# A gated-linear-attention and dilated-window decoder trunk: the elementwise work of the seven-product pairs on VectorE alone

## The chip, the cores and the metric

The kernel runs on one core of one Trainium2 chip. The metric is the device time of one execution in microseconds (us), as the median of several runs. Profiles are of one execution, taken by the hardware profiler. The engines are called PE (TensorE, the matrix engine; PEld is its loading of weights), DVE (VectorE), ACT (ScalarE), POOL (GpSimd) and SP (SyncE, which here only issues DMAs).

## The reference

The program is a decoder trunk of two layers for one sequence of 1024 tokens with 1024 features, in float32. The first layer is gated linear attention with four heads, the second is dilated sliding-window attention with eight query heads in three groups of window and dilation over one shared K and V. Cut to what matters here:

```
proj = x @ w_in                        # layer 1: q, k, v, g and the gates' low rank part
o = gla_chunked(q, k, v, log_a)
x = layer_norm(ALPHA * x + (rms(o) * norm_g * silu(g)) @ w_out)
k, v = split(x @ w_kv); k = rope(k)    # shared by all of layer 2
q, g = split(x @ w_in2); q = rope(q)   # three groups x eight heads of 128
o = softmax-weighted sum over the groups of dilated_window_attention(q, k, v)
x = layer_norm(ALPHA * x + (o * silu(g)) @ w_out2)
```

The matrix products that the change concerns are some of the projections `x @ w`: q and k of all heads of layer 1, and in layer 2 the shared K and most of the q.

## The kernel before

**Precision.** TensorE takes float32 operands in a rounded form (fp32r) at a higher pace than whole float32. A projection is therefore done with split operands: every operand x is stored as a rounded high part and a low part x - high, and a product is three matmuls: high x high, high x low and low x high. ScalarE makes the high part (`split_hi`), and a subtraction makes the low part (`split_lo`, which may go to VectorE or GpSimd). For some weights the low part is made otherwise: ScalarE writes the negative high part, and a DMA issued by GpSimd adds the weight to it in memory (`accum_op`).

**Seven products for a pair.** Two projections of the same input that belong together (q and k of a head, or two K or q heads) are one pair. Such a pair is a 2 x 2 block product: two output blocks of features by two halves of the sequence, over two halves of the input features. It is computed with seven block products in place of eight (P1 to P7), at the price of sums of weight blocks before, and additions of results after. The sums of the input blocks (T1 to T4) are made once per layer. For each pair, `load_pair` (from line 783) loads the two weights (tiles `wf`), forms four sums of weight blocks (tiles `sum`: t1 to t4, by `total`), and splits them with `put` into high parts (`wh`) and low parts (`wl`; the last pair of tiles is called `s`). `seven` (from line 831) issues the 84 matmuls of 128x512 into four PSUM tiles (all called `sev` in the profile), copies P1 and P7 out with ScalarE (u1 and u2, in the profile `u<-sev`), because P2 and P4 are added onto the same banks afterwards, and forms the results: with VectorE `f += P5`, `u += P6`, `c21 = u + (P7 + P4)` and `u += P3`, and last `f = u + f` (`u<-u,u`), on whichever of VectorE and GpSimd the planner picks. There are four pairs in layer 1 and fourteen in layer 2 (three for K, eleven for q; list `EARLY`). In layer 2 each result is turned by `rope` (tiles `t` and `pair`), in layer 1 it is stored to DRAM (`c`, `u`).

**What sets the order.** The program is written as a list of operations, and a planner (class `Sched`, `order`, from line 270) plays them through before anything is issued: it has a price for every operation on every engine, knows which tiles each reads and writes, how many buffers a tile has and a priority, and takes the operation that can start first. `S.vector`, `S.scalar` and so on are one engine; `S.vp` leaves the planner the choice between VectorE and GpSimd, `S.va` between VectorE and ScalarE, `S.vap` among all three. Each engine then runs its own queue in the planned order, and waits at an operation until what it reads is there. An operation that moves to another engine therefore changes the planned times of what follows, and with them the order of the queues and the later choices for other `S.vp` and `S.vap` operations. All instructions have one line in the profile (line 469, where the planner issues them), so they are told apart by their tiles.

**The rest.** After the pairs of layer 2 comes the attention of the eight heads (tiles `P`, `PT`, `lv`, `po`, `nat`, `og`), in which TensorE also does the remaining q projections and the g projections (`acc`), then the output projection with the layer norm.

Of the kernel before, what the change touches and what calls it, by code (L numbers as in the profile page):

```python
# [7 lines left out]
F32 = mybir.dt.float32  # L8
# [116 lines left out]
class Pool:  # L125
# [6 lines left out]
    def tile(self, shape, dtype, name, tag=None, bufs=1):  # L132
        b = Buf(self, shape, dtype, name, tag or name, bufs)
        self.bufs_made.append(b)
        cols = int(_np.prod(shape[1:]))
        if self.space == "DRAM":
            idx = _np.arange(int(_np.prod(shape))).reshape(shape)
        else:

            idx = _np.broadcast_to(_np.arange(cols).reshape((1,) + tuple(shape[1:])), shape)  # L140
        return View(b, idx)
# [484 lines left out]
def trunk(tc, xT, xp, wP, wA, wA12, wAv3, w2, wO, wK, wV0, wV12, wB, wOB, par_d,  # L626
          ident_d, lmask_d, cos_d, sin_d, bmask_d, rmask_d, tri_d, lnr_d, out):
    S = Sched(tc, lat=LAT, pad=PAD)
# [8 lines left out]
    t2 = S.pool("t2", after=(tq,))  # L637
    t0 = S.pool("t0", side="right")
    t1 = S.pool("t1", side="right", after=(t0,))
# [3 lines left out]
    def split_hi(dst, src):  # L643
        S.scalar.activation(dst, src, AF.Copy)

    def split_lo(dst, src, hi):
        S.vp.tensor_sub(dst, src, hi.bitcast(F32))

    def page(pool, dt, name):
        return pool.tile([128, T], dt, name=name, tag="pg", bufs=16)  # L650
# [4 lines left out]
    def hs(half):  # L655
        return slice(half * 512, half * 512 + 512)
# [112 lines left out]
    def og_page(kt, pool):  # L769
        while kt >= len(ogs):  # L770
            n = len(ogs)
            a = page(pool, FR, f"ogh{n}")
            b = page(pool, FR, f"ogl{n}")
            ogs.append((a, b))
        return ogs[kt]

    def pairs(xs, quarter, tile):
        L, R = slice(0, 512), slice(512, 1024)

        def four(x):  # L780
            return x.rearrange("p (k c) -> p k c", k=4)

        def load_pair(src, first=False):
            with S.later(-WEIGHTS):
                a, b = (wts.tile([128, 1024], F32, name="wf", bufs=2) for _ in range(2))
                for x, w in ((a, src[0]), (b, src[1])):
                    S.sync.dma_start(x.rearrange("p (k c) -> p k c", k=NK), w)

                def halves():
                    hi, lo = (wts.tile([128, 1024], FR, name=n, bufs=3) for n in ("wh", "wl"))  # L790
                    return [(hi[:, c], lo[:, c]) for c in (L, R)]

                def put(w, x, more=None):
                    hi, lo = w
                    split_hi(hi, x)
                    if more is None:
                        split_lo(lo, x, hi)
                    else:
                        S.scalar.activation(lo, x, AF.Copy, scale=-1.0)
                        S.gpsimd.dma_start(four(lo), more, accum_op=OP.add)  # L800
                    return four(hi), four(lo)

                def total(op, x, y):
                    t = tile("sum", "a")
                    op(t, x, y)
                    return t

                w0, w1 = halves()
                a11 = put(w0, a[:, L], None if first else src[0][:, 0:4])
                t3 = total(S.vp.tensor_sub, a[:, L], b[:, L])  # L810
                s3 = put(w1, t3)
                w0, w1 = halves()
                a12 = put(w0, a[:, R], None if first else src[0][:, 4:8])
                a22 = put(w1, b[:, R], None if first else src[1][:, 4:8])
                w0, w1 = halves()
                t1 = total(S.vp.tensor_add, b[:, L], b[:, R])
                s1 = put(w0, t1)
                t2 = total(S.vp.tensor_sub, t1, a[:, L])
                s2 = put(w1, t2)
                t4 = total(S.vp.tensor_sub, a[:, R], t2)  # L820
                s4 = put([tile("s4", "d", FR) for _ in range(2)], t4)
            return dict(P1=a11, P2=a12, P4=a22, P7=s3, P5=s1, P6=s2, P3=s4)

        def pure(k0, h):
            return [(xs[k0 + k][0][:, hs(h)], xs[k0 + k][1][:, hs(h)]) for k in range(4)]

        MOVING = dict(P1=lambda: pure(0, 0), P2=lambda: pure(4, 0), P3=lambda: pure(4, 1),
                      **{p: lambda n=n: [quarter(n, k) for k in range(4)]
                         for p, n in (("P4", "T4"), ("P5", "T1"), ("P6", "T2"), ("P7", "T3"))})

        def seven(w, evac):
            banks = {}

            def prod(p, bank):
                first = bank not in banks
                if first:
                    tag = {"a": "acc", "b": "lv", "c": "po", "d": "acc"}[bank]
                    banks[bank] = ps.tile([128, 512], F32, name="sev", tag=tag, bufs=2)
                acc = banks[bank]
                hi, lo = w[p]  # L840
                for k, (xh, xl) in enumerate(MOVING[p]()):
                    with S.group():
                        S.tensor.matmul(acc, hi[:, k, :], xh, start=first and k == 0, stop=False, skip_group_check=True)
                        S.tensor.matmul(acc, hi[:, k, :], xl, start=False, stop=False, skip_group_check=True)
                        S.tensor.matmul(acc, lo[:, k, :], xh, start=False, stop=(k == 3), skip_group_check=True)
                return acc

            def late():
                return S.later(-EVAC)

            acc = prod("P1", "a")
            u = tile("u1", "a")
            with S.later(-WEIGHTS - EVAC):
                S.scalar.copy(u, acc)
            acc = prod("P7", "b")
            f = tile("u2", "a")
            with S.later(-WEIGHTS - EVAC):
                S.scalar.copy(f, acc)
            acc = prod("P2", "a")
            with late():  # L860
                evac(0, 0, acc)
            prod("P4", "b")
            acc = prod("P5", "c")
            with late():
                S.vector.tensor_add(f, f, acc)
            acc = prod("P6", "d")
            with late():
                S.vector.tensor_add(u, u, acc)
                c21 = tile("c", "a")
                S.vector.tensor_add(c21, u, banks["b"])  # L870
                evac(1, 0, c21)
                S.vp.tensor_add(f, u, f)
                evac(1, 1, f)
            acc = prod("P3", "c")
            with late():
                S.vector.tensor_add(u, u, acc)
                evac(0, 1, u)

        return load_pair, seven

    def natural(x):
# [981 lines left out]
    def quarter(name, k):  # L1863
        pg = QS.setdefault((name, k), page(p0, FR, f"{name}{k}"))
        return pg[:, 0:512], pg[:, 512:1024]
# [44 lines left out]
    for half in range(2):  # L1910
        for kt in range(4, 6):
            load_og(ogB[kt], kt, p1, lambda: small("ogf", "a", NA), (half,))
        for u in (6, 7):
            hi, lo = og_page(u, p1)
# [8 lines left out]
    for kt in range(NK):  # L1923
        wf = wts.tile([128, 1024], F32, name="wf", bufs=2)
        q = p1 if kt < 4 else p0
        hi, lo = page(q, FR, "woh"), page(q, FR, "wol")
# [116 lines left out]
```

## Time and profile before

| | |
|---|---|
| median of 3 runs | 1106.04 us (1105.65 to 1107.79) |
| the profiled execution | 1106.84 us |
| its span, first to last instruction | 1105.1 us |
| mean granted TensorE clock | 0.999 |
| busy: PE / DVE / ACT / POOL | 1092.1 / 884.8 / 653.4 / 215.5 us |

A line of a group reads: line, engine, operation, out<-in by the program's names (buffer numbers left out), shapes, count | busy time in us, mean ns of one | idle time of the engine just before them, and what ended it. `wl<-sum,wh` is the low part of a sum of weights, `u<-u,u` the last addition. A line of the timeline has the start in us from the span's start, the duration in us, the engine and the operation, and in brackets for how long the engine was idle before it and what it waited for. A line of the waits has the engine and the tile that waited, what it waited for, the total in us, how often, and the longest.

### The profile page before, as it was taken

How to read it: one execution, taken by the hardware profiler on the slowest of the kernel's cores; microseconds unless marked ns; L12 is line 12 of the kernel's file. 1: busy time of each engine (PE TensorE's matmuls, PEld its weight loads, DVE VectorE, ACT ScalarE, POOL GpSimd, SP SyncE). 2: the span in 40 equal slices, each digit the busy share in tenths (PEclk: the TensorE clock that was granted, in tenths of full speed). 3: DMA queues.
4: the chain of work that ended last, by engine and by line, in shares of the span. 5: the costliest groups of instructions: out<-in, count | busy, mean ns of one | idle time of the engine just before them, and what ended most of it. 6: DMA issues, size and time to landing. Idle time of an engine off the chain costs nothing.

```text
span 1105.1 us, 20222 instructions
## 1 busy us (share of the span) xinstructions
PE 1092.1 (99%) x7532; PEld 932.7 (84%) x7532; DVE 884.8 (80%) x1786; ACT 653.4 (59%) x1330; POOL 215.5 (19%) x247
## 2 busy tenths in 40 slices
PE   9999999999999999999999999999999999999997
PEld 9978888888888888888887888888888898888886
DVE  5886879999567589888888989885588878786578
ACT  5565545666455255656666666675677787763252
POOL 0121100000013021012223322111133553340010
PEclk9999999999999999999999999999999999999999
DMA  8467783134362455767756776678533553241644
GB/s 301 140 211 201 242 290 124 65 134 165 107 202 90 148 166 196 228 175 159 183 151 178 184 203 169 186 189 273 167 97 124 194 160 103 99 152 64 188 136 176
DMA packets 92626, 185.70 MB, mean 168 GB/s; under 512 B 16912, under 2 KB 38032, under 8 KB 92528
## 3 DMA queue, kind: packets, MB, share of 16 engines
q1 hardware_dynamic: 84320, 167.11, 46.1%
q0 software_dynamic: 8208, 17.31, 9.2%
q8 instruction: 59, 0.97, 0.4%
q14 instruction: 39, 0.32, 0.1%
HBM read 134.57 MB, written 47.71 MB: 165 GB/s over the span
## 4 chain that ended last, share of the span: by engine, by line
PE 89%; DVE 5%; DMA 3%; issue 1%; ACT 1%; POOL 0%; DVEq 0%; POOLq 0%; ACTq 0%; SPq 0%
PE acc L469 28%; PE sev L469 26%; PE po L469 12%; PE lv L469 9%; PE vac L469 8%; PE ms L469 4%; PE pro L469 3%; DMA wf<-in_wB 1%; DMA wf<-in_wOB 1%; DVE pair L469 1%; DMA wf<-in_wA 1%; DVE sum L469 1%; DVE wl L469 1%; DVE P L469 1%; DVE xg L469 1%
## 5 line engine op out<-in xcount | busy, mean ns | idle before, releaser
L469 ACT ACTIVATE wh<-wf 128x1024 fp32r<-128x1024 f32 (+3 forms) x118 | 99.5, 844 | 98.6 <-PE acc L469 37.0
L469 PE MATMUL sev<-T,wh 128*128 128x512 f32 x448 | 137.8, 389 | 0.0
L469 PEld LDWEIGHTS sev<-T,wh 128*128 128x128 f32 x448 | 84.1, 188 | 17.4
L469 PE MATMUL sev<-T,wl 128*128 128x512 f32 x224 | 87.2, 389 | 0.0
L469 PE MATMUL lv<-K,Q 128*64 128x64 f32 (+2 forms) x512 | 72.1, 287 | 0.6 <-DVE nat L469 0.5
L469 PE MATMUL acc<-x1h,wh 128*128 128x512 f32 x160 | 71.2, 445 | 0.0
L469 DVE TENSOR_TENSOR wl<-wf,wh 128x1024 fp32r<-128x1024 f32 (+3 forms) x55 | 62.2, 1135 | 10.9 <-ACT wh L469 10.7
L469 POOL DMA_DIRECT2D wl<-in_wB x42 | 36.9, 882 | 169.4 <-ACT wl L469 152.2
L469 DVE CUSTOM_DVE_ANT_0 P<-lv,bmask 128x256 f32<-128x256 f32 (+1 forms) x128 | 47.6, 379 | 19.4 <-PE lv L469 16.9
L469 PE MATMUL acc<-x1h,wl 128*128 128x512 f32 x160 | 62.8, 392 | 0.0
L469 PE MATMUL acc<-x1l,wh 128*128 128x512 f32 x160 | 62.5, 391 | 0.0
L469 POOL TENSOR_TENSOR wl<-wf,wh 128x1024 fp32r<-128x1024 f32 x7 | 16.7, 2388 | 234.3 <-PE ms L469 195.4
L469 DVE TENSOR_TENSOR pair<-t,t 128x512 f32<-128x512 f32 x56 | 60.3, 1083 | 0.3
L469 PEld LDWEIGHTS lv<-K,Q 128*128 128x128 f32 (+1 forms) x512 | 51.8, 164 | 8.8 <-DVE nat L469 1.0
L469 DVE TENSOR_TENSOR t<-t,sinT 128x512 f32<-128x512 f32 x60 | 43.1, 720 | 15.0 <-ACT t L469 14.8
L469 ACT ACTIVATE P<-P,sts 128x64 f32<-128x64 f32 (+2 forms) x128 | 49.8, 391 | 8.5 <-DVE sts L469 7.3
L469 PE MATMUL acc<-xh,wh 128*128 128x512 f32 x128 | 52.6, 411 | 0.0
L469 DVE TENSOR_TENSOR u<-u,sev 128x512 f32<-128x512 f32 x54 | 36.5, 683 | 17.8 <-PE sev L469 17.5
L469 PE MATMUL acc<-xh,wl 128*128 128x512 f32 x128 | 50.1, 391 | 0.0
L469 PE MATMUL acc<-xl,wh 128*128 128x512 f32 x128 | 49.9, 390 | 0.0
L469 PEld LDWEIGHTS sev<-T,wl 128*128 128x128 f32 x224 | 42.0, 188 | 8.8
L469 ACT ACTIVATE t<-u 64x512 f32<-64x512 f32 x56 | 35.4, 632 | 20.8 <-DVE u L469 17.3
(346 smaller groups left out, 3379.9 us busy)
## 6 DMA issues: line engine op xcount, KB each, us to landing
wf<-in_wB SPq DMA_DIRECT2D x32, 512.0 KB, 6.2
wf<-in_wA SPq DMA_DIRECT2D x24, 512.0 KB, 4.1
qd<-pair SPq DMA_DIRECT2D x22, 512.0 KB, 3.2
Q<-qd SPq DMA_DIRECT2D x22, 512.0 KB, 7.9
wl<-in_wB POOLq DMA_DIRECT2D x33, 256.0 KB, 7.1
wf<-in_wO SPq DMA_DIRECT2D x16, 512.0 KB, 3.3
wf<-in_wOB SPq DMA_DIRECT2D x16, 512.0 KB, 3.7
wf<-in_wV SPq DMA_DIRECT2D x10, 512.0 KB, 4.2
```

The costliest lines, as they stand in the source:

```text
L469: getattr(handle[o.eng], meth)(*[conv(a) for a in args], **{k: conv(v) for k, v in kw.items()})
```

## The change

Six lines in `load_pair` and `seven` name VectorE in place of the choice between VectorE and GpSimd; in a pair they issue nine operations: the four sums of weights, the low parts that are made by a subtraction (the four of the sums; in a layer's first pair three more, of plain weights), and the final addition `f = u + f`. The other uses of `S.vp` and of `split_lo` in the program stay. The planner, its prices and everything else are the same; the planner runs anew on the changed list.

```diff
                     if more is None:
-                        split_lo(lo, x, hi)
+                        S.vector.tensor_sub(lo, x, hi.bitcast(F32))
...
-                t3 = total(S.vp.tensor_sub, a[:, L], b[:, L])
+                t3 = total(S.vector.tensor_sub, a[:, L], b[:, L])
...
-                t1 = total(S.vp.tensor_add, b[:, L], b[:, R])
+                t1 = total(S.vector.tensor_add, b[:, L], b[:, R])
                 s1 = put(w0, t1)
-                t2 = total(S.vp.tensor_sub, t1, a[:, L])
+                t2 = total(S.vector.tensor_sub, t1, a[:, L])
                 s2 = put(w1, t2)
-                t4 = total(S.vp.tensor_sub, a[:, R], t2)
+                t4 = total(S.vector.tensor_sub, a[:, R], t2)
...
-                S.vp.tensor_add(f, u, f)
+                S.vector.tensor_add(f, u, f)
```

Both programs hold the same operations, the same DMAs and the same 84 matmuls a pair. What moves is the engine of some of them and, through the planner, the order of the queues. First GpSimd's queue in the pairs of the second layer, before; `in_wK` and `in_wB` are the weights of K and of q, the DMAs are those that add onto low parts, and `u`, `wl`, `sum` and `s` are operations that the diff touches:

```order
L469 TENSOR_TENSOR wl<-sum,wh 128x512 x2
L469 TENSOR_TENSOR sum<-wf 128x512
L469 DMA wl<-in_wB 128x512 x3
L469 TENSOR_TENSOR u_6372<-u_6367,u_6372 128x512
L469 DMA wl<-in_wB 128x512 x3
L469 TENSOR_TENSOR s_6625<-sum,s_6607 128x512
```

These six rows are a piece from the fifth to the seventh pair. GpSimd's queue after, over all fourteen pairs and what stands next to them:

```order
L469 TENSOR_TENSOR T_5414<-rt,T_5414 128x512
L469 DMA wl<-in_wK 128x512 x6
L469 DMA wl<-in_wB 128x512 x33
L469 DMA wl<-in_wB 128x1024
L469 MEMSET diag 128x512 x2
L469 DMA wl<-in_wB 128x1024 x2
```

The computation between the DMAs has left the queue. ScalarE's queue in the sixth pair of the second layer, before; `u_6367` and `u_6372` are the copies of P1 and P7, `wh<-sum` is the rounding of a sum of the next pair's weights:

```order
L469 ACTIVATE wh<-wf 128x512
L469 ACTIVATE wl<-wf 128x512
L469 ACTIVATE wh<-sum 128x512
L469 ACTIVATE u_6367<-sev 128x512
L469 ACTIVATE u_6372<-sev 128x512
L469 ACTIVATE s_6385<-sum 128x512
```

The rounding stands ahead of the copies. The same place after, where the copies are `u_6363` and `u_6371`:

```order
L469 ACTIVATE wh<-wf 128x512
L469 ACTIVATE wl<-wf 128x512
L469 ACTIVATE u_6363<-sev 128x512
L469 ACTIVATE u_6371<-sev 128x512
L469 ACTIVATE wh<-sum 128x512
L469 ACTIVATE s_6377<-sum 128x512
```

The copies have moved ahead of the rounding. In the fourth pair of the second layer it went the other way; ScalarE's queue there before, with the copies `u_6010` and `u_6016`:

```order
L469 ACTIVATE wh<-wf 128x512
L469 ACTIVATE wl<-wf 128x512
L469 ACTIVATE u_6010<-sev 128x512
L469 ACTIVATE u_6016<-sev 128x512
L469 ACTIVATE wh<-sum 128x512
L469 ACTIVATE s_6023<-sum 128x512
```

The copies stand first. The same place after, where the copies are `u_6023` and `u_6027` and `t_5991` belongs to the rope of the pair before:

```order
L469 ACTIVATE wh<-wf 128x512
L469 ACTIVATE wl<-wf 128x512
L469 ACTIVATE wh<-sum 128x512
L469 ACTIVATE t_5991<-u_5834 64x512
L469 ACTIVATE u_6023<-sev 128x512
L469 ACTIVATE u_6027<-sev 128x512
L469 ACTIVATE s_6034<-sum 128x512
```

The rounding, and a piece of the rope, have moved ahead of the copies.

## The prediction, made before the changed kernel ran

> **What bounds the kernel now.** I read the page's first part, then TensorE's waits, then busy time by stretches, then the groups of GpSimd and VectorE, and last the timeline around the one wait of TensorE that the change can touch. The page:
>
> ```profile
> span 1105.1 us, 20222 instructions
> PE 1092.1 (99%) x7532; PEld 932.7 (84%) x7532; DVE 884.8 (80%) x1786; ACT 653.4 (59%) x1330; POOL 215.5 (19%) x247
> ```
>
> TensorE is busy for 1092.1 of 1105.1 us. Moving elementwise work among the other engines can therefore win at most the 13.0 us in which TensorE is not busy. All its waits, from the table of waits:
>
> ```profile
> PE lv L469 <- issue: 1.4, 2, 1.1
> PE pro L469 <- DVE zero L469: 1.3, 1, 1.3
> PE sev L469 <- ACT u L469: 1.2, 1, 1.2
> PE vac L469 <- issue: 0.7, 1, 0.7
> PE lv L469 <- DVE nat L469: 0.5, 1, 0.5
> PE sev L469 <- DVE tT L469: 0.5, 1, 0.5
> ```
>
> They sum to 5.6 us, and the stretches place most of the rest:
>
> ```profile
> 490.00:760.00 270.00, 268.77 (x1188) 221.87 (x1187) 233.24 (x325) 171.30 (x292) 64.81 (x63) 1.00 0.71 185
> 800.00:1000.00 200.00, 199.38 (x1439) 178.62 (x1436) 162.89 (x659) 148.48 (x507) 84.41 (x132) 1.00 0.41 129
> 1000.00:1105.00 105.00, 97.69 (x460) 81.56 (x459) 73.25 (x110) 37.25 (x54) 5.08 (x3) 0.99 0.45 148
> ```
>
> The columns are length, then busy time and count of PE, PEld, DVE, ACT and POOL, then clock and DMA. The last 105 us hold 7.3 us without TensorE, mostly the final layer norm and store, which run after the last seven-product. From 490 to 760 us, where the fourteen pairs of the second layer run, TensorE is idle for 1.2 us in all. The attention (800 to 1000 us) has 0.6 us.
>
> Matmul busy time could hide slow matmuls, so I also count them, in slices of 20 us:
>
> ```profile
> 560.00:580.00 20.00, 20.00 (x90) 16.57 (x89) 16.00 (x24) 12.87 (x23) 5.13 (x5) 1.00 0.56 146
> 580.00:600.00 20.00, 18.83 (x84) 15.22 (x83) 18.19 (x23) 12.64 (x22) 6.89 (x6) 1.00 0.63 172
> 600.00:620.00 20.00, 20.00 (x90) 16.57 (x89) 17.64 (x26) 13.06 (x23) 4.67 (x5) 1.00 0.77 191
> ```
>
> A full slice issues 90 matmuls, one in 0.222 us. The middle slice issues 84, which makes the loss 6 x 0.222 = 1.33 us, against 1.17 us of missing busy time.
>
> **Where that wait comes from.** The timeline of four engines, each line with its start, its duration and what it waited for:
>
> ```profile
> 584.62 2.89 POOL L469 TENSOR_TENSOR wl<-sum,wh 128x512 fp32r<-128x512 f32 x2
> 584.94 3.55 DVE L469 TENSOR_TENSOR pair<-t,t 128x512 f32<-128x512 f32 x1
> 592.43 0.69 DVE L469 TENSOR_TENSOR sum<-wf 128x512 f32<-128x512 f32 x1 [1.43 <-DMA wf<-in_wB]
> 592.54 1.74 POOL L469 TENSOR_TENSOR sum<-wf 128x512 f32<-128x512 f32 x1 [5.03 <-DMA wf<-in_wB]
> 594.31 0.63 ACT L469 ACTIVATE wh<-sum 128x512 fp32r<-128x512 f32 x1 [1.55 <-POOL sum L469]
> 594.85 1.07 ACT L469 ACTIVATE u<-sev 128x512 f32<-128x512 f32 x2
> 593.92 0.39 PE L469 MATMUL sev<-T,wl 128*128 128x512 f32 x1
> 595.48 0.50 PE L469 MATMUL sev<-x1h,wh 128*128 128x512 f32 x1 [1.17 <-ACT u L469]
> ```
>
> The weights land at about 592.4 us. VectorE forms one sum in 0.69 us and GpSimd the other in 1.74 us. ScalarE stands at the rounding of GpSimd's sum (wh), and behind it in its queue are the two copies (u) that take P1 and P7 out of their banks. P2 adds onto P1's bank, so TensorE waits 1.17 us for the copy. This is the only place in the trace where a GpSimd operation of this code reaches TensorE.
>
> **The change part by part.** First, what leaves GpSimd. These groups of the whole program are the code that the diff touches:
>
> ```profile
> L469 POOL TENSOR_TENSOR u<-u,u 128x512 f32<-128x512 f32 x8 | 12.0, 1506 | 14.7 <-DVE u L469 14.7
> L469 POOL TENSOR_TENSOR wl<-sum,wh 128x512 fp32r<-128x512 f32 x8 | 11.1, 1442 | 4.9 <-ACT wh L469 4.9
> L469 POOL TENSOR_TENSOR sum<-wf 128x512 f32<-128x512 f32 x3 | 4.5, 1511 | 13.0 <-DMA wf<-in_wB 5.0 <-issue 4.4 <-DMA mq<-c 3.5
> L469 POOL TENSOR_TENSOR s<-sum,s 128x512 fp32r<-128x512 f32 x2 | 3.0, 1498 | 2.2 <-ACT s L469 2.2
> L469 POOL TENSOR_TENSOR sum<-wf,sum 128x512 f32<-128x512 f32 x2 | 2.6, 1301 | 13.9 <-DVE sum L469 13.9
> L469 POOL TENSOR_TENSOR sum<-sum,wf 128x512 f32<-128x512 f32 x1 | 1.3, 1292 | 5.4 <-DVE sum L469 5.4
> ```
>
> That is 8 + 8 + 3 + 2 + 2 + 1 = 24 operations and 34.5 us of GpSimd; the planner had given VectorE all others already. What they cost on VectorE, and what VectorE pays for their neighbourhood today:
>
> ```profile
> L469 DVE TENSOR_TENSOR pair<-t,t 128x512 f32<-128x512 f32 x56 | 60.3, 1083 | 0.3
> L469 DVE TENSOR_TENSOR t<-t,sinT 128x512 f32<-128x512 f32 x60 | 43.1, 720 | 15.0 <-ACT t L469 14.8
> L469 DVE TENSOR_TENSOR wl<-sum,wh 128x512 fp32r<-128x512 f32 x46 | 37.1, 825 | 1.2 <-ACT wh L469 1.2
> L469 DVE TENSOR_TENSOR sum<-wf 128x512 f32<-128x512 f32 x33 | 23.6, 755 | 9.2 <-DMA wf<-in_wB 7.1 <-DMA wf<-in_wK 1.4 <-DMA wf<-in_wA 0.7
> L469 DVE TENSOR_TENSOR t<-u,cosT 128x512 f32<-128x512 f32 x28 | 20.4, 728 | 0.0
> L469 DVE TENSOR_TENSOR t<-c,cosT 128x512 f32<-128x512 f32 x14 | 11.5, 822 | 0.2
> L469 DVE TENSOR_TENSOR c<-u,sev 128x512 f32<-128x512 f32 x18 | 12.3, 683 | 2.6 <-PE sev L469 2.2
> ```
>
> The last group reads PSUM and takes 683 ns; that is the undisturbed price, so the additions cost 24 x 0.683 = 16.4 us. The groups with both inputs in SBUF have higher means. The pair<-t,t of the timeline shows why: it began during GpSimd's wl operations (584.62 to 587.51 us), ended about 1.0 us after them, and took 3.55 us instead of 1.08 us. The excess over 683 ns is 46 x 0.142 = 6.5 (wl), 33 x 0.072 = 2.4 (sum), 14 x 0.139 = 1.9, 60 x 0.037 = 2.2 and 28 x 0.045 = 1.3 us, and 2.5 us for that one pair: 16.8 us. If all of it goes, VectorE's load changes by 16.4 - 16.8 = -0.4 us; if none goes, by +16.4 us. I take -0.4, since the pair's row shows the cause directly. Even +16.4 us would fit: from 490 to 760 us, where most of it falls, VectorE is idle for 36.8 us. So VectorE does not become the bound. The Trainium skill's "Perfetto Trace Analysis" (Optimizing Scalar/DVE Operations) speaks against the change as far as VectorE is saturated: then giving work to GpSimd may make sense. The trace has VectorE at 233.24 of 270 us there, which is not saturated; if it were, the 16.4 us would come on top of the time. The Trainium skill's "SBUF — State Buffer" (SBUF: two separate sides) says that a VectorE operation with two SBUF inputs and a reading GpSimd operation exclude each other for a whole instruction; the pair's row agrees. By that rule VectorE could get back as much as the 34.5 us that GpSimd held, and would end 18 us lighter; as VectorE is not the bound, the time would be the same.
>
> GpSimd's issues of the accumulating DMAs (wl<-in_w...), which bring the other low parts, now wait behind no computation: in the rows of its queue shown with the change, everything between the DMAs is gone. I cost this at nothing: TensorE never waits for such a DMA in its table, and an earlier issue only lengthens the cover.
>
> Second, the planner moves ScalarE's queue. In the sixth pair of the second layer, the place of the 1.17 us wait, the rows with the change show the copies (u_6367 before, u_6363 after) behind the rounding before, and ahead of it after. So this wait goes whole: -1.2 us (between -1.33 by the count and 0 if something else is late there). But over the fourteen pairs the rounding stands ahead of the copies 9 times before and 10 times after: the fourth, eighth and tenth pair lose the good order that the third and sixth gain. What the rounding waits for there is a landing:
>
> ```profile
> DVE sum L469 <- DMA wf<-in_wB: 7.1, 5, 1.7
> ```
>
> VectorE waited five times for late weights, and one of the five reached TensorE, with GpSimd's slow sum on top. Each of the ten places can thus cost between 0 and 1.2 us. I take a third of one such wait, +0.4 us: the sum itself is now 0.69 instead of 1.74 us, so the landing that cost 1.2 us before would cost 1.2 - 1.0 = 0.2 us at such a place now.
>
> Third, the attention. The shifted start makes the planner deal again there: GpSimd has 107 instead of 91 of the scalings and maskings of P (P and PT below), 8 instead of 12 of og<-og,sg and 5 instead of 7 full-width wl, and VectorE and ScalarE what is left.
>
> ```profile
> L469 POOL TENSOR_SCALAR P<-P,ew 128x256 f32<-128x256 f32 x27 | 14.1, 551 | 4.0 <-DVE ew L469 4.0
> L469 POOL TENSOR_SCALAR P<-P,cw 128x256 f32<-128x256 f32 x9 | 5.7, 637 | 0.0
> L469 POOL TENSOR_TENSOR PT<-P,ident 128x256 f32<-128x256 f32 x9 | 7.5, 843 | 2.8 <-PE po L469 2.6
> ```
>
> Sixteen more at 0.55 to 0.84 us are 9 to 13 us, on an engine that is idle for 115 of these 200 us. TensorE's idle time there was 0.6 us, so little can be won; 1.5 us either way is my estimate from the six waits above, whose size is 0.5 to 1.4 us. I take 0.
>
> Sum: -1.2 + 0.4 + 0 = -0.8 us. The profiled execution took 1106.84 us, 1.74 us above its span and 0.8 us above the median of 1106.04 us; it becomes 1106.0 us, and the median 1105.2 us. The runs before spread over 2.1 us, so about 0.2% (2.2 us) is what can be told from no change, and the forecast is: no change.
>
> **The rivals.** *Slower: late weights meet the new queues.* If three of the ten places where a rounding stands ahead of the copies get a wait of 1.2 us, and the old one goes, that is -1.2 + 3.6 = +2.4 us: 1108.4 us. It decides from the third such wait on. For it: five late landings in this trace, and three pairs that changed to the bad order. Against it: four of the five cost nothing, and every sum now takes 0.69 us. A new wait for P in several of the eight attention rounds would act on top.
>
> *Faster: hidden stalls go too.* If besides the 1.2 us the waits for nat and tT (0.5 us each) go, that is 2.2 us, and any relief in the attention takes it beyond: 1103.6 us. For it: VectorE loses operations of up to 3.55 us that made its queue late. Against it: TensorE's count is full in the slices beside the wait.
>
> *The change does nothing.* The old wait could stay with another cause: 1106.0 us, within the forecast's band.
>
> **How the numbers follow.** No change within 0.2%: 0.70, of which the forecast's own mechanism has 0.55 and "does nothing" 0.15. Faster: 0.15, since nearly every recoverable wait must go. Slower: 0.15, since three new waits are needed, and the queues of the pairs and of the attention have both moved. The range runs from 1103.3 us (faster rival with 0.3 us more) to 1107.8 us (two new waits of 1.2 us, 1107.2, and 0.6 us of the attention's doubt); it leaves out about 1 in 10 at each end.
>
> **What would show it.** Right: POOL has none of the six groups; wl<-sum and sum<-wf on VectorE have means near 685 ns; VectorE's total stays within some 5 us of 884.8 us, while GpSimd's falls by about 30 us; TensorE shows no wait for u near 594 us and its busy total stays within 2 us of 1092.1 us. Wrong: waits "PE sev <- ACT u" at three or more places, a slice of the pairs with under 88 matmuls, or waits of lv or po for POOL in the attention.

## The result and the profile after

The kernel after takes 1113.38 us (median of 5 runs, 1111.4 to 1113.84), the kernel before 1106.06 us in the same series. The ratio is 1.0064, with a 95% interval of 1.0052 to 1.0075: slower, where no change was forecast. The same code measured again later (e11 below) gave 1111.08 us and 1.0051 (1.0036 to 1.0067). So the change costs 5 to 7 us.

The page of the profiled execution, which took 1113.31 us:

```profile
span 1111.5 us, 20202 instructions
PE 1092.7 (98%) x7532; PEld 932.0 (84%) x7532; DVE 878.4 (79%) x1795; ACT 653.9 (59%) x1334; POOL 182.6 (16%) x234
```

The work is about what the prediction said: TensorE has the same 1092.7 us (1092.1 before), GpSimd lost 32.9 us, and VectorE, with 24 operations more to do in the pairs, is 6.4 us lighter. What grew is the time in which TensorE is idle, from 13.0 to 18.8 us. Its largest waits now:

```profile
PE sev L469 <- ACT u L469: 3.9, 3, 2.8
PE lv L469 <- issue: 3.3, 3, 1.6
...
PE vac L469 <- issue: 1.0, 1, 1.0
```

The wait for the copies `u` was one of 1.2 us; now there are three, and one is 2.8 us. Busy time by stretches (the columns are those of the prediction's stretches), first two of before that the prediction did not read:

```profile
62.00:135.00 73.00, 72.52 (x319) 59.33 (x317) 57.45 (x86) 43.91 (x72) 15.80 (x16) 1.00 0.72 208
135.00:310.00 175.00, 172.97 (x2561) 146.33 (x2559) 147.34 (x252) 97.34 (x138) 2.37 (x1) 1.00 0.42 149
```

And of after:

```profile
62.00:135.00 73.00, 70.18 (x308) 57.32 (x307) 54.23 (x86) 41.98 (x68) 10.08 (x12) 1.00 0.69 202
135.00:310.00 175.00, 170.74 (x2549) 144.37 (x2548) 146.22 (x249) 95.96 (x134) 2.37 (x1) 1.00 0.42 148
490.00:760.00 270.00, 268.56 (x1201) 221.63 (x1200) 231.17 (x345) 171.78 (x296) 36.70 (x43) 1.00 0.71 183
```

The loss is in layer 1: TensorE has 2.3 us less in the stretch of the four pairs (62 to 135 us) and 2.2 us less in the one behind it. The second figure belongs for the most part to this one execution: in e11, the same code, TensorE has 172.89 us there, 0.1 us less than before. The stretch on which the prediction spent its words, 490 to 760 us, moved by 0.2 us. That the neighbours of GpSimd got shorter shows in VectorE's groups of after:

```profile
L469 DVE TENSOR_TENSOR pair<-t,t 128x512 f32<-128x512 f32 x56 | 56.1, 1003 | 0.5
L469 DVE TENSOR_TENSOR wl<-sum,wh 128x512 fp32r<-128x512 f32 x54 | 36.5, 705 | 3.6 <-ACT wh L469 3.6
L469 DVE TENSOR_TENSOR sum<-wf 128x512 f32<-128x512 f32 x36 | 24.4, 717 | 11.5 <-DMA wf<-in_wB 8.3 <-DMA wf<-in_wK 3.2
```

The means fell from 1083, 825 and 755 ns, and eight low parts more cost 0.6 us less in sum (37.1 to 36.5).

**Where the 2.8 us come from.** The second pair of layer 1, in the timeline of before:

```profile
69.62 0.42 SPq L469 DMA_DIRECT2D mq<-c  x1
...
74.53 0.75 DVE L469 TENSOR_SCALAR mn<-z,par 128x512 f32<-128x512 f32 x1 [0.47 <-ACT sp L469]
75.20 0.68 DVE L469 TENSOR_TENSOR u<-u,sev 128x512 f32<-128x512 f32 x1
...
77.04 1.50 POOL L469 TENSOR_TENSOR sum<-wf 128x512 f32<-128x512 f32 x1 [3.54 <-DMA mq<-c]
78.17 0.60 ACT L469 ACTIVATE u<-sev 128x512 f32<-128x512 f32 x1 [1.49 <-DMA mq<-u]
```

And of after:

```profile
68.53 0.33 SPq L469 DMA_DIRECT2D mq<-c  x1
...
76.66 0.75 DVE L469 TENSOR_SCALAR mn<-z,par 128x512 f32<-128x512 f32 x1 [3.47 <-DMA mq<-c]
77.33 0.68 DVE L469 TENSOR_TENSOR sum<-wf 128x512 f32<-128x512 f32 x1
77.93 0.68 DVE L469 TENSOR_TENSOR u<-u,sev 128x512 f32<-128x512 f32 x1
...
80.91 0.68 DVE L469 TENSOR_TENSOR_SCAN b<-smask,mn 128x256 f32<-128x256 f32 x1
81.69 0.60 ACT L469 ACTIVATE u<-sev 128x512 f32<-128x512 f32 x1 [6.43 <-DVE b L469]
82.34 0.50 PE L469 MATMUL sev<-xh,wh 128*128 128x512 f32 x1 [2.82 <-ACT u L469]
```

The tiles `sum`, `u`, `c`, `sp` and `mn` of layer 1 share nine buffers (kind `a`). One of them is held by `c` until its store `mq<-c` has landed, which by the rows takes 7.4 us from its issue before and 8.1 us after. Before, GpSimd's sum got this buffer, waited 3.54 us for it, and had nothing behind it that anybody missed. After, the same wait (3.47 us) is at the head of VectorE's queue, at `mn`, a step of the gates. Behind it stand the moved sum, the evacuation of P3 (`u<-u,sev`, at 77.93 instead of 75.20 us) and the scans `b`. The copy of the next pair's P1 (`u<-sev` on ScalarE) now gets the buffer of a `mn`, which a scan frees, and starts 3.5 us later than before. TensorE stands still for it.

**The second place.** A burst of small matmuls in the attention of layer 1 (64 rows `lv<-X` in the order, 128 records in the profile), in TensorE's timeline of before:

```profile
182.18 1.41 PE L469 MATMUL lv<-X 128*32 128x32 f32 x128
```

And of after, where the planner has put the burst ahead of two triples of `acc` matmuls that it stood behind:

```profile
183.13 1.20 PE L469 MATMUL lv<-X 128*32 128x32 f32 x108
185.43 0.38 PE L469 MATMUL lv<-X 128*32 128x32 f32 x20 [1.10 <-issue]
```

TensorE stops after 108 of the 128 for 1.10 us and waits for nothing that the profile shows.

**Layer 2.** In the sixth pair the copies stand ahead of the rounding, and the wait near 594 us is gone. In the twelfth the rounding waits for a sum and the copies wait behind it. There ScalarE has the rounding ahead of the copies in both kernels; what differs is VectorE's queue. Before, the sums came ahead of a step of the rope:

```profile
708.17 1.34 DVE L469 TENSOR_TENSOR sum<-wf 128x512 f32<-128x512 f32 x2
709.38 0.74 DVE L469 TENSOR_TENSOR t<-t,sinT 128x512 f32<-128x512 f32 x1
```

After, VectorE works without a break and reaches them only behind that step and a `pair<-t,t`, 1.8 us of work:

```profile
712.75 0.74 DVE L469 TENSOR_TENSOR t<-t,sinT 128x512 f32<-128x512 f32 x1
713.53 1.11 DVE L469 TENSOR_TENSOR pair<-t,t 128x512 f32<-128x512 f32 x1
714.56 1.29 DVE L469 TENSOR_TENSOR sum<-wf 128x512 f32<-128x512 f32 x2
715.28 0.63 ACT L469 ACTIVATE wh<-sum 128x512 fp32r<-128x512 f32 x1 [2.07 <-DVE sum L469]
716.45 1.06 ACT L469 ACTIVATE u<-sev 128x512 f32<-128x512 f32 x2
717.07 0.50 PE L469 MATMUL sev<-x1h,wh 128*128 128x512 f32 x1 [0.61 <-ACT u L469]
```

All this is put together in a table of how far TensorE is behind the kernel before. Both traces hold 7532 matmuls; an entry is the start of the n-th in the trace named, less the start of the n-th in the trace of before, where n is the matmul that starts at the time above the column in before. A jump between two columns is time lost in between; the end is that of the last matmul. A TensorE that is late can find a later wait shorter (e1 between 592 and 607 us), so the jumps of a row do not simply add up.

| us | 73 | 90 | 192 | 497 | 592 | 607 | 757 | 990 | end |
|---|---|---|---|---|---|---|---|---|---|
| after | -1.1 | 2.0 | 3.6 | 4.4 | 5.6 | 4.1 | 5.4 | 6.6 | 6.5 |
| after again (e11) | -1.0 | 2.5 | 2.7 | 2.8 | 2.9 | 1.4 | 2.6 | 3.8 | 3.3 |
| layer 1 only (e1) | -1.2 | 3.9 | 4.8 | 4.5 | 4.6 | 3.5 | 3.4 | 3.4 | 2.9 |
| layer 2 only (e2) | -0.3 | -0.3 | -0.6 | -0.1 | 0.4 | -1.1 | 0.1 | 0.9 | 1.3 |
| order of before (e3) | 0.2 | 3.3 | 3.3 | 3.6 | 3.5 | 2.4 | 2.1 | 2.0 | 2.1 |
| all but one sum (e4) | -1.0 | -0.2 | -0.5 | 2.5 | 2.7 | 1.5 | 1.1 | 1.1 | 1.0 |
| sum behind P3 (e5) | -1.7 | 0.1 | 0.0 | 0.2 | 0.4 | -0.5 | -0.9 | -1.8 | -2.3 |
| thrice (e6) | -1.5 | -0.1 | -0.4 | 2.4 | 6.4 | 8.2 | 10.3 | 9.5 | 8.9 |
| ten buffers (e7) | -1.4 | -1.4 | -0.8 | -0.6 | 0.2 | -1.3 | -0.5 | 0.4 | -0.4 |
| before, ten buffers (e8) | -0.6 | 0.4 | 0.4 | 0.5 | 0.5 | 0.5 | 0.5 | -0.4 | -0.3 |
| evacuation first (e9) | 0.2 | 0.2 | 1.0 | 1.1 | 1.9 | 0.4 | 1.4 | 2.3 | 2.0 |
| and burst back (e10) | -0.7 | -0.7 | -0.9 | -0.5 | -0.3 | -1.8 | -0.6 | 0.2 | -0.8 |
| one sum (e12) | -1.4 | -1.4 | -1.8 | -1.5 | -0.6 | -1.6 | -1.7 | -2.6 | -2.7 |

### The profile page after: what moved, and what is told of

It is laid out like the page before. It is cut to its first block, busy times and chain, and to the rows that moved or that the text cites. A ratio compares the mean times of both kernels' runs of the same rounds, so it can differ in the third digit from the quotient of the medians.

```text
span 1111.5 us, 20202 instructions
## 1 busy us (share of the span) xinstructions
PE 1092.7 (98%) x7532; PEld 932.0 (84%) x7532; DVE 878.4 (79%) x1795; ACT 653.9 (59%) x1334; POOL 182.6 (16%) x234
## 5 line engine op out<-in xcount | busy, mean ns | idle before, releaser
L469 DVE TENSOR_TENSOR wl<-wf,wh 128x1024 fp32r<-128x1024 f32 (+3 forms) x57 | 64.6, 1138 | 13.2 <-ACT wh L469 13.0
L469 PEld LDWEIGHTS lv<-K,Q 128*64 128x64 f32 (+1 forms) x512 | 51.8, 164 | 9.9 <-issue 1.4
L469 DVE TENSOR_TENSOR pair<-t,t 128x512 f32<-128x512 f32 x56 | 56.1, 1003 | 0.5
L469 POOL TENSOR_TENSOR wl<-wf,wh 128x1024 fp32r<-128x1024 f32 x5 | 11.9, 2390 | 229.1 <-PE ms L469 193.2
L469 PE MATMUL acc<-ogh,wh 128*128 128x512 f32 x120 | 47.4, 395 | 0.0
```

What stands on the lines that cost most here:

```text
L469: getattr(handle[o.eng], meth)(*[conv(a) for a in args], **{k: conv(v) for k, v in kw.items()})
```

## The experiments

The theory: the cost is the place of a few instructions in their queues, in layer 1 above all. The rival: VectorE's added work costs it. In each run "before" was timed beside the others; its medians were 1105.9 to 1106.7 us. The edits are shown in short; a name such as `layer1_sum` or `o.moved` stands for a test in the run's own code.

**Which layer?** e1 and e2 make the change in the pairs of one layer only; the other keeps the choice.

```diff
-    def pairs(xs, quarter, tile):
+    def pairs(xs, quarter, tile, vp):      # vp stands for S.vector in the six lines of the change
...
-        load_pair, seven = pairs(xs, quarter, front)
+        load_pair, seven = pairs(xs, quarter, front, S.vector)   # e1; e2: S.vp
...
-        load_pair, seven = pairs(xs, quarter, lambda name, kind, dt=F32: small(...))
+        load_pair, seven = pairs(xs, quarter, lambda name, kind, dt=F32: small(...), S.vp)   # e1; e2: S.vector
```

> Only the four pairs of layer 1 name VectorE; layer 2 has the choice again and keeps the orders of before. Theory (queues): the loss of layer 1 comes whole, about 3.1 us at the second pair (a VectorE instruction waits for a buffer that a store of c frees, the evacuation of P3 stands behind it, and ScalarE's copy u behind that) and about 2.4 us of issue waits of TensorE between 173 and 300 us, where bursts of 32x32 matmuls have moved together: 1111 us. Rival (load): each operation that moves to VectorE costs its share; 4 of 24 move, so about 1.2 us: 1107.3 us.

> Only the fourteen pairs of layer 2 name VectorE; everything ahead of 490 us is as before. Theory (queues): 1.0 us net in the pairs (old wait near 594 us gone, two or three smaller ones come) and about 1 us in the attention and the tail: 1108 us, with no change at all ahead of 490 us. Rival (load): 20 of 24 operations, so 6 us: 1112 us.

e1: 1109.85 us (1109.31 to 1111.72), ratio 1.0039 (1.0024 to 1.0054). e2: 1107.37 us (1105.94 to 1108.11), ratio 1.0006 (0.9995 to 1.0016). Of the 24 moved operations four are in layer 1 (two low parts, one sum, one addition), and these bring more than half of the loss, with the long wait in e1's table:

```profile
PE sev L469 <- ACT u L469: 3.2, 1, 3.2
```

The other twenty, of layer 2, bring nothing that can be told from zero. If VectorE's work cost the time, it would be the other way round. The 2.4 us of issue waits that I expected from e1 did not come: its row gains 0.6 us from 90 to 497 us. Of its 5.1 us from 73 to 90 us only 3.2 are the wait; the rest is a lower clock (see the last section).

**The same work in the old order.** In e3 the planner still chooses between VectorE and GpSimd, so every queue is planned as before; only when it is done are its 24 operations for GpSimd handed to VectorE. e4 does the same with 23 of them and leaves layer 1's one sum (the one that waited 3.54 us) on GpSimd. e5 is e3 with this sum placed one row further back in VectorE's queue, behind the evacuation of P3.

```diff
         done.sort(key=lambda o: (o.t0, o.seq))
+        for o in done:
+            if o.pair: o.eng = "DVE"        # pair: recorded by load_pair or seven as VectorE or GpSimd
...
+            if o.pair and not layer1_sum(o): o.eng = "DVE"     # e4
...
+        layer1_sum.t0 = just behind u<-u,sev                   # e5, ahead of the sort
```

> The planner plans with the choice as before, and only when the instructions are issued the 24 operations that it gave to GpSimd are put into VectorE's queue at their planned places; all orders are otherwise those of before, TensorE's whole. Theory (queues): the sum of layer 1's second pair now stands in VectorE's queue ahead of the evacuation of P3 and waits there for the store of c, as in the changed kernel, so 2 to 3 us are lost near 79 us; no new issue waits, since TensorE's order is the old one; the old wait near 594 us shrinks by about half. 1107.5 us. Rival 1 (load): 1112 us or more. Rival 2 (the new orders alone are to blame): 1105 us, nothing lost near 79 us.

> As the run before, but the one sum of layer 1 that GpSimd formed stays on GpSimd; 23 of the 24 operations run on VectorE. Theory (queues): the 2 to 3 us near 79 us go, and the half of the old wait near 594 us stays won: 1105.3 us. Rival 1 (load): within 0.3 us of the run before.

> As the kernel planned as before with the 24 operations run on VectorE (e3), but in VectorE's queue one weight sum of layer 1's second pair (sum<-wf, near 77 us) stands behind the evacuation of the third product (u<-u,sev) instead of ahead of it; all other queues are as in e3, and all 24 operations stay on VectorE. Theory (that sum waits for a buffer that the store mq<-c frees, and the evacuation stood behind it): TensorE's wait near 79 to 80 us is at most 1 us instead of 3.1, the run about 1105.5 us. Rival (VectorE's added 16 us of work, or its contention, costs the time): the wait and the time stay as in e3, about 1108 us.

e3: 1108.06 us (1106.99 to 1111.23), ratio 1.0019 (1.0010 to 1.0028). e4: 1105.22 us (1103.6 to 1109.36), ratio 1.0003 (0.9992 to 1.0014). e5: 1105.64 us (1104.51 to 1108.14), ratio 1.0001 (0.9990 to 1.0011). The times are those that the theory gave, within 0.6 us, and e5 says it most plainly: with all 24 operations on VectorE, two neighbours in one queue that change places are worth about 2 us. In the two traces the place itself is worth 1.3 us (from 73 to 90 us e3 loses 3.1, e5 1.8). And the timelines correct the theory. In e3:

```profile
77.90 0.75 DVE L469 TENSOR_SCALAR mn<-z,par 128x512 f32<-128x512 f32 x1 [3.39 <-DMA mq<-c]
79.17 0.68 DVE L469 TENSOR_TENSOR u<-u,sev 128x512 f32<-128x512 f32 x1
82.93 0.60 ACT L469 ACTIVATE u<-sev 128x512 f32<-128x512 f32 x1 [5.41 <-DVE b L469]
```

In e5:

```profile
76.26 0.75 DVE L469 TENSOR_SCALAR mn<-z,par 128x512 f32<-128x512 f32 x1 [3.72 <-DMA mq<-c]
76.93 0.68 DVE L469 TENSOR_TENSOR u<-u,sev 128x512 f32<-128x512 f32 x1
79.78 0.60 ACT L469 ACTIVATE u<-sev 128x512 f32<-128x512 f32 x1 [4.24 <-DMA mq<-u]
```

I had written that the moved sum waits for the buffer. In both it is `mn` that waits, as in after, and e4's shows the same though its sum is on GpSimd. What the swap changes is the rest of the chain: the evacuation comes 0.6 us sooner behind `mn`, and the copy on ScalarE again gets the buffer that the store `mq<-u` frees, as before, and not one that a scan frees. TensorE's wait for that copy in e5 is still 1.6 us, where I had expected at most 1 us. So the wait went to VectorE's queue because other tiles get the buffers there, and not because the sum brought it along: in e4 it came with the other three operations of layer 1. Why `mn` gets that buffer, no run shows.

**Is VectorE's load free, then?** e6 is e4 with the 15 moved operations that do not write over their input executed three times. Every value stays the same.

```diff
-                    getattr(handle[o.eng], meth)(...)
+                    for _ in range(3 if o.moved and not o.in_place else 1):
+                        getattr(handle[o.eng], meth)(...)
```

> As the kernel with 23 of the 24 operations on VectorE and the one sum of layer 1 left on GpSimd (e4), but 15 of the moved operations (those that do not write over their own input) are executed three times, 30 added operations of about 0.69 us: 20 us more of VectorE's time in the pairs. Theory (it is the place in a queue that costs, not the load): within 1.5 us of e4, about 1105 to 1106.5 us. Rival (the load of the moved operations costs time): 1110 us or more.

1117.54 us (1115.76 to 1119.08), ratio 1.0103 (1.0088 to 1.0118). My expectation failed: it costs 12 us against e4, of which the lower clock of the last section can be a part. In its trace 7.9 us of the 8.9 us lie between 497 and 757 us. The page:

```profile
PE 1093.6 (98%) x7532; PEld 933.6 (84%) x7532; DVE 900.7 (81%) x1839; ACT 653.3 (59%) x1330; POOL 183.9 (17%) x224
```

Its waits:

```profile
PE sev L469 <- ACT u L469: 7.3, 6, 3.0
PE sev L469 <- DVE u L469: 1.5, 2, 1.2
```

And the pairs of layer 2 among its stretches:

```profile
490.00:760.00 270.00, 262.30 (x1162) 215.43 (x1162) 244.34 (x366) 168.99 (x291) 35.57 (x40) 1.00 0.67 174
```

VectorE is idle there for 25.7 us and TensorE still loses 6.5 us more than before, in waits of up to 3.0 us at the copies: the added operations stand in chains (sum, rounding, copy, TensorE) and lengthen them by up to 1.4 us for each operation executed thrice (30 executions added 20.5 us over e4's 880.2 us, 0.68 us each). So idle time of VectorE in a stretch does not make work there free. Two things can have spared the change this price, and no run separates them. VectorE's neighbours became shorter: 900.7 us is within 1 us of what it would have had (884.8 + 16.4 = 901.2 us) without that, and it had 881.5 us in e5 and 878.4 in after. And a moved operation takes 0.7 us in place of 1.3 to 1.5 on GpSimd, so the change shortens the chains that e6 lengthens.

**More buffers.** e7 is after with ten buffers of kind `a` and, to make room, three of kind `d`; e8 is before with the same.

```diff
-NA, NA0 = 12, 9
+NA, NA0 = 12, 10
...
-            return t0.tile([128, 512], dt, name=name, tag=kind, bufs={"a": NA0, "d": 4}[kind])
+            return t0.tile([128, 512], dt, name=name, tag=kind, bufs={"a": NA0, "d": 3}[kind])
```

> The kernel after, with ten a buffers of layer 1's pairs instead of nine (and three d buffers instead of four, to make room). Theory: the wait of VectorE near 77 us for the store mq<-c goes or moves behind the evacuation, and TensorE's 3.2-us gap near 79 us with it: about 1110 us; what is left over the kernel before are the waits of the small matmuls' new order near 184 us and of layer 2. Rival (the gap has another cause than the buffer): about 1113 us.

> The control: the kernel before with the same ten a and three d buffers. There the wait for mq<-c stands in GpSimd's queue and nobody waits for it. Theory: within 1 us of the kernel before, 1105 to 1107 us. Rival (the buffers by themselves are worth 3 us): about 1103 us.

e7: 1105.95 us (1105.09 to 1109.96), ratio 1.0003 (0.9994 to 1.0013): the whole loss is gone, more than the 3 us expected. e8: 1108.37 us (1106.32 to 1111.34), ratio 1.0020 (1.0010 to 1.0029): before gets slower by it, so the buffers are not worth 7 us by themselves. In e7's timeline:

```profile
73.53 0.68 DVE L469 TENSOR_TENSOR u<-u,sev 128x512 f32<-128x512 f32 x1
76.49 0.75 DVE L469 TENSOR_SCALAR mn<-z,par 128x512 f32<-128x512 f32 x1 [1.67 <-DMA mq<-c]
78.92 1.07 ACT L469 ACTIVATE u<-sev 128x512 f32<-128x512 f32 x2
```

`mn` still waits for the store. But the planner, which counts one buffer more, has put the evacuation ahead of it, and the copies start at 78.92 us without a wait. This asks for the order alone.

**The order alone.** e9 is after with the evacuation moved up two rows in VectorE's queue, ahead of the waiting `mn`; all other queues are after's, row by row (below are rows of that queue, not code). e10 also puts the burst of small matmuls back behind the two triples of `acc`, where it stands before. e11 is after, unchanged, on the same chip.

```diff
 L469 TENSOR_SCALAR mn<-z,par 128x512
+L469 TENSOR_TENSOR u_833<-u_833,sev 128x512
 L469 TENSOR_SCALAR mn<-z,par 128x512
 L469 TENSOR_TENSOR sum<-wf 128x512
-L469 TENSOR_TENSOR u_833<-u_833,sev 128x512
```

> The kernel after with one instruction of VectorE's queue moved up by two places: in layer 1's second pair the evacuation of the third product (u<-u,sev, near 77.9 us) stands ahead of the step mn<-z,par that waits for the store mq<-c, and of the sum behind it. Every other queue and row is the kernel after's; all 24 operations stay on VectorE. Theory A (additive: that place costs the 3.2-us gap near 79 us and nothing else): TensorE's gap there falls under 0.5 us and the run comes to 1113.4 - 3.1 = about 1110.3 us. Theory B (the lost time of the bursts of small matmuls follows from the moment at which they are reached, so it falls too, as with ten buffers): 1106 to 1108 us. Rival (the moved load): 1113 us.

> As the kernel after with the evacuation moved up (e9), and on TensorE the burst of 64 small matmuls lv<-X near 184 us put back behind the two triples of acc, as it stands in the kernel before. Theory (the place of that burst costs the new issue wait there): the 1.3-us wait at 184 us goes, and the run is 1 to 1.5 us under e9. Rival (the issue waits come and go by execution, not by place): within 0.5 us of e9.

> The kernel after, unchanged, beside the two runs above on the same chip: is its time the same on another day and chip? Expected: 1113 us (1111.5 to 1114), with TensorE's 3.2-us gap near 79 us. If it comes to 1109 to 1110 us, a part of the distance to the kernel with ten buffers belongs to the executions and not to the code.

e11: 1111.08 us (1110.15 to 1115.22), ratio 1.0051 (1.0036 to 1.0067). e9: 1107.82 us (1105.78 to 1111.54), ratio 1.0013 (1.0004 to 1.0023). e10: 1106.51 us (1105.02 to 1109.05), ratio 1.0010 (1.0001 to 1.0019). One instruction moved up by two rows wins 3.3 us of the 5.1; this is theory A's 3.1 us, though my 1110.3 us came out wrong because the first series of after lies 2.3 us above its second. By its time alone e9 would fit theory B too; but in its trace the burst of small matmuls still loses 0.83 us, which B did not expect. In e9's timeline:

```profile
74.67 0.69 DVE L469 TENSOR_TENSOR u<-u,sev 128x512 f32<-128x512 f32 x1 [0.24 <-PE sev L469]
77.96 0.75 DVE L469 TENSOR_SCALAR mn<-z,par 128x512 f32<-128x512 f32 x1 [2.60 <-DMA mq<-c]
79.16 0.60 ACT L469 ACTIVATE u<-sev 128x512 f32<-128x512 f32 x1 [2.67 <-DMA mq<-u]
```

VectorE still waits 2.60 us for the store, and TensorE does not notice. The burst in e11:

```profile
183.06 1.20 PE L469 MATMUL lv<-X 128*32 128x32 f32 x108
184.53 0.38 PE L469 MATMUL lv<-X 128*32 128x32 f32 x20 [0.28 <-issue]
```

And in e10, whole again:

```profile
181.29 1.36 PE L469 MATMUL lv<-X 128*32 128x32 f32 x128
```

In the five traces with after's order (after, e1, e7, e9, e11) the burst breaks at the same matmul, for 1.10, 0.83, 0.55, 0.83 and 0.28 us; in none of the nine with before's order does it break. The place is shown, its price is not: e10 is 1.3 us under e9, but the intervals overlap.

**The term of the prediction by itself.** e12 is before with one operation handed to VectorE: the `sum<-wf` of layer 2's sixth pair.

```diff
         done.sort(key=lambda o: (o.t0, o.seq))
+        sixth_pair_sum.eng = "DVE"      # 1 of the 24
```

> The kernel before, planned as before, with one of the 24 operations run on VectorE: the sum<-wf of layer 2's sixth pair (1.74 us on GpSimd, near 592 us), the one whose lateness TensorE waits for near 594 us. The other 23 stay on GpSimd. It measures the term of the prediction by itself: the 1.2-us wait near 594 us goes, TensorE reaches 607 us about 1.2 us earlier, and the run is 1104.8 us. Rival (the wait has another releaser, or comes back behind the next product): TensorE's place at 607 us is unchanged, 1106 us.

1105.11 us (1103.83 to 1107.44) against 1106.67 us of before beside it, ratio 0.9988 (0.9979 to 0.9997): the one version that is faster than both kernels, though by less than the 0.2% that I had set as the bound. Its timeline:

```profile
591.99 1.29 DVE L469 TENSOR_TENSOR sum<-wf 128x512 f32<-128x512 f32 x2 [1.57 <-DMA wf<-in_wB]
592.72 0.64 ACT L469 ACTIVATE wh<-sum 128x512 fp32r<-128x512 f32 x1 [0.54 <-DVE sum L469]
593.89 0.50 PE L469 MATMUL sev<-x1h,wh 128*128 128x512 f32 x1 [0.22 <-ACT u L469]
```

The wait of 1.17 us is 0.22 us, and the table has 1.0 us won between 592 and 607 us. But 0.8 us is lost in the pair ahead of it (between 497 and 592 us), so this trace nets 0.2 us in layer 2's pairs. The 1.4 us that e12 has already won at 73 us belong to the execution, not to the edit: most traces have them.

## Why the prediction was wrong

**The step that failed** is the costing of the move in layer 1. The prediction priced the 24 operations as load ("24 x 0.683 = 16.4 us", set off against 16.8 us that come back), took the one GpSimd operation that TensorE waits for before the change as the place that matters, and then looked for new waits in ScalarE's queue in layer 2 alone. The waits that VectorE's queue would get there, and what stands behind them, it put at nothing without a look. The sign was in a row that it quoted: three `sum<-wf` on GpSimd, with 3.5 us of waiting for the DMA `mq<-c`. That wait cost nothing on an engine with nothing behind it. In after the wait for the same store stands on VectorE, at `mn` and not at the moved sum, with the evacuation behind it. That is 3.1 us of after (from -1.1 to 2.0 in the table), 3.3 us by e11 against e9.

**The order of TensorE's queue** was not looked at. The burst near 184 us adds 0.3 to 1.1 us by the waits shown.

**The sixth pair** was right in mechanism and size: -1.2 us forecast, 1.5 us won from 592 to 607 us in e2, where TensorE comes to it nearly on time, 1.0 us in e12. The 1.5 us of after prove less: e1, which leaves this pair as it was, wins 1.1 us there, because TensorE comes 4.6 us later than before and the weights only 3.5 us.

**The new waits of layer 2** were looked for at the wrong place and priced too low: +0.4 us forecast, for late weights at a place such as the fourth, eighth and tenth pair, where ScalarE's order turned bad. No trace of the new order has a wait above 0.14 us at these three. The wait that came in every newly planned trace, 0.5 to 0.6 us in the twelfth pair, has ScalarE's old order and comes from VectorE's queue. Smaller ones (at most 0.5 us) came in the first and the last pair. From 497 to 757 us the six kernels whose layer 2 is planned anew (after, e2, e7, e9, e10, e11) end between -0.2 and +1.0 us by the table; those in the old order that hand over all the operations of layer 2 (e3, e4 and e5) win 1.5, 1.4 and 1.1 us. So the new order gives back 1 to 2.5 us, and nothing is left of the forecast net gain of 0.8 us.

**The attention** was put at 0 with 1.5 us either way. From 757 to 990 us the same six kernels lose 0.8 to 1.2 us; e1, e3, e5 and e12, with the old order there, lose none. The size is inside the bound; which of the operations dealt anew makes the loss, no run shows.

**VectorE's load**: the relief of its neighbours was right in kind (878.4 us, 6.4 us below before, where -0.4 was forecast). In e3 and e5, where nothing else changes its engine, it is 881.8 and 881.5 us; so about 3 us are relief, and the other 3 came with the new deal. The Trainium skill's "SBUF — State Buffer" (SBUF: two separate sides), by which a VectorE operation with two SBUF inputs and a reading GpSimd operation exclude each other, allowed more relief than I took, and the trace agrees with it in direction. But "Even +16.4 us would fit" does not follow from idle time: e6 paid 12 us for 20.5 us.

**The rivals.** The slower one had the sign and not the cause: it needed late weights at three places, and what cost most was one late buffer in layer 1. Its sign, waits for `u` at three or more places, stood in the first trace (three) and not in e11's (two). Its time, 1108.4 us, was 5.0 us short of the first series and 2.7 us of the second.

**What stays open:** why ten buffers win 1.9 us more than e9 and e10's 0.5 us above before; why e8 is slower, since its one trace, of 1106.56 us, shows no loss; and by what rule the buffer of `c` goes to `mn`. The lower clock of the last section can be a part of the first two; how large a part was not measured.

## What to carry to other kernels

When operations move to another engine, waits can turn up in its queue, even at operations that were there before. Read what the moved ones waited for where they were, also where it cost nothing so far, and then what would stand behind such a wait at the new place. A small operation that waits for a buffer belongs on an engine that nobody waits for, or behind the evacuations. And price a chain, not a total: 20 us, on an engine that still had 26 us to spare, cost 12.

## What was not expected of the hardware

TensorE can stop inside a burst of very small matmuls with nothing to wait for in the profile: 128 of them in 1.4 us ran whole or broke after 108, by where they stand in the program, for 0.28 to 1.10 us. Such issue waits also differ between executions of one code: 4.3 us in all in the first trace of after, 2.1 us in e11's. The Trainium skill's "Runtime: NRT & Kernel Launch" (Instruction fetch mechanics) says that instructions are fetched in blocks by a DMA queue of the engine's own and that the cost is mostly hidden; the fixed place of the break fits blocks, and if the fetch is the cause, its cost showed here. That it is the cause was only argued.

A wait of TensorE can also cost more than its length. In e1's trace the granted clock (the figure behind the five engines) is 0.50 from 84.14 to 87.55 us, 1.5 us after the end of the 3.24-us wait:

```profile
84.20:87.50 3.30, 3.30 (x9) 2.58 (x8) 1.49 (x3) 1.53 (x3) 0.88 (x1) 0.50 0.98 366
```

The same length of 3.41 us at 0.50 follows issue waits of 2.50 and 2.48 us near 294 us in e4's and e6's traces. Half of it, 1.7 us, is an estimate of what each costs; e1 loses 1.9 us from 73 to 90 us beside its wait. It does not follow always: after, e11 and e3 have waits of 2.8, 3.2 and 2.7 us in their traces, and e6 one of 2.95 us, with full clock behind them. The mean clocks of the three executions are 0.997, 0.996 and 0.997. As low a mean was granted in 4 of 5 executions of after's first series, 3 of 6 of e11, 5 of 10 of e3, 4 of 4 of e6, 4 of 10 of e8 and 3 of 11 of e9 and of e10 each, but in 3 of 90 of before and in none of e2, e5 and e7. So distances between the medians can hold a part that comes from this clock; where it fell in the executions without a trace is not on record.
